# The two seams of a two-phase feed-forward: where x1 is stored from, when weights and blocks are loaded, and which buffers hold them

## The chip, the cores and the metric

The kernel runs on one core of a Trainium2 chip. The metric is device time in microseconds, from the start to the end of one execution. The core has a matrix engine (PE in the profile), a vector engine (DVE), a scalar engine (ACT), a general engine (POOL) and an engine that here only issues transfers (SP). Every engine works through its own queue in order; transfers that SP issues run on 16 DMA engines beside the others.

## The reference, cut to what matters

One layer of a streaming encoder over 1024 prompt frames and 64 sample frames (1088 tokens), model width 1024. The convolution branch, the memory branch and their merge come first; the change touches what follows:

```python
x1 = layer_norm(ALPHA * x + merged @ w_out, ln1_g, ln1_b)
ff = jnp.square(jax.nn.relu(x1 @ w_ff1)) @ w_ff2          # 1024 -> 4096 -> 1024
x2 = layer_norm(ALPHA * x1 + ff, ln2_g, ln2_b)
```

All is float32. A product is made of three passes over operands split in a high and a low part (`mm3`: high times high, high times low, low times high), so every operand has to be split once: ACT makes the high part, DVE subtracts it from the source (`split`).

## The kernel before

**Who sets the order.** The kernel is written as a Python program over symbolic tiles. A planner turns it into one fixed queue per engine: it walks a clock of its own, and whenever an engine is free in that clock it takes, among the instructions whose inputs and buffers are ready, the one that stands earliest in the program. An instruction that is ready early can so be queued far ahead of its place in the program. `pin` keeps single instructions in program order. All transfers of the kernel are issued by SP. A pool hands its buffers round; a tile waits for the last reader of the bytes that it takes over.

**Norm and first seam.** `out_proj` (L857) goes over three token chunks of 384, 384 and 320 tokens, with eight products each. For each product a slice `sx` of x is loaded back from memory (L866) and added by DVE (L872). `ln1(ci)` (L836) runs in the background, one step per product: it leaves x1 of a chunk in three tiles, the high part in pool `ph`, the low part in pool `pl` (both with three buffers, one per chunk) and the full value `Y2` in pool `f`. At its end it stores all three to memory, `y1D`, `x1Dh`, `x1Dl` (L852), because the phases after it need other shapes.

The feed-forward has 32 hidden row blocks. Four of them, units u = 0 to 3, are made the plain way (`first_units`, `unit`), 24 matmuls for each chunk, and `post_h` (L914) makes relu squared with one ACT and one DVE instruction, splits it, and stores high and low part to `hidDh`, `hidDl` (L922). Its tiles come from a ring of four (`ztile`, pool `hvs1`). Meanwhile `x1_sums` (L927) makes the four sums t1 to t4 that the fast scheme below needs, split in high and low parts, in six steps of eight DVE instructions; its two work tiles come from the same ring.

**Phase one** (`ff_first`, L1017) makes the other 28 hidden row blocks as 14 pairs (quads), q = 0 to 13. Each is a 2x2 block product in seven products instead of eight, P1 to P7. P1, P2 and P3 read parts b11, b21 and b22 of x1, which are loaded from `x1D` into the buffers of `ph` and `pl` (six transfers `xb`, L1024, in the order b11, b22, b21); P5, P6, P7 and P4 read t1, t2, t3 and t4. The order on PE is, per turn q: P6(q-1), P1(q), P7(q-1), P5(q), P4(q-1), P2(q), P3(q). The weights of a quad come as one transfer `raw` of 1 MB into a single buffer (pool `rawp`, L1037), the buffer that before held the third unit's weights; `produce` splits them in seven items, in a ring of nine (`ws`, pool `f`). ACT and DVE make seven result tiles a quad, again split, and store them to `hvD` (`put`, L1090): the operands of phase two, already in its form.

**Phase two** (`ff_second`, L1168) multiplies by `w_ff2` in seven blocks of two quads of phase one each; a block has four quads of its own (28 in all), each with seven products of twelve matmuls of 272 columns. A block's 14 operand tiles `hv` are loaded from `hvD` (`load_hv`, L1220) into one of two pools, `hvp0` for even and `hvp1` for odd blocks. The pools take bytes that phase one held. The weights of a quad are loaded by `load_w` (two buffers), split by `split_w` (three buffers). The result is accumulated by DVE in four tiles `YF` (L1244), which start as ALPHA times x1, loaded from `y1D` (L1262). The four hidden blocks of the units are multiplied at the end (`last_ff2`): `last_weights` (L1274) loads and splits their four weight tiles at the end of block 5, together with the eight halves of `hidD`. `last_ff2` turns `YF` to token-major, adds the last product, and does the final norm and the stores.

Of the kernel before, what the change touches and what calls it, by code (L numbers as in the profile page):

```python
# [9 lines left out]
F32 = mybir.dt.float32  # L10
# [39 lines left out]
def hybrid_layer(ctx, tc, x_prompt, x_sample, cache_conv, state_C, state_n, state_m, w_in, b_gate,  # L50
# [15 lines left out]
    base = ExitStack()  # L66
    ph = pool("ph", 3, stack=base)
    pl = pool("pl", 3, stack=base)
    fp = pool("f", 3, stack=base)
# [15 lines left out]
    hidD = [dram.tile([4 * P, T], F32, name=f"hidD{e}") for e in "hl"]  # L85
# [750 lines left out]
    def ln1(ci):  # L836
# [13 lines left out]
        o = CHUNKS[ci][0]  # L850
        for dst, src in ((y1D, Y2[ci]), (x1D[0], X1H[ci].bitcast(F32)), (x1D[1], X1L[ci].bitcast(F32))):
            nc.sync.dma_start(dst[:, o:o + n].rearrange("(k p) t -> p k t", p=P), src[:, :, :n])  # L852
        if ci == 2:
            lnq.close()
            lns.close()

# [57 lines left out]
    def post_h(u):  # L914
        def f(ci, o, n, ps):
            r, hi = ztile("r"), ztile("rh")
            rf = r.bitcast(F32)
            S.activation(rf[:, :n], ps[:, :n], AF.Relu)
            V.scalar_tensor_tensor(rf[:, :n], ps[:, :n], 0.0, rf[:, :n], ALU.max, ALU.mult)
            split(hi[:, :n], r[:, :n], rf[:, :n])  # L920
            for e, t in enumerate((hi, r)):
                nc.sync.dma_start(hidD[e][u * P:(u + 1) * P, o:o + n], t.bitcast(F32)[:, :n])  # L922
        return f
# [3 lines left out]
    def x1_sums():  # L927
# [4 lines left out]
        def rows(kh, i, ci, o, n):  # L932
            return Y2[ci][:, 4 * i + kh:4 * i + 4:2, o:o + n]

        for a, b, ca, oa, cb, ob in ((0, 224, 0, 0, 1, 160), (224, 384, 0, 224, 2, 0), (384, 544, 1, 0, 2, 160)):
            n = b - a
            for i in range(2):
                b11, b21, b12, b22 = rows(0, i, ca, oa, n), rows(1, i, ca, oa, n), rows(0, i, cb, ob, n), rows(1, i, cb, ob, n)
                z = [ztile("xs").bitcast(F32)[:, :2 * n].rearrange("p (k t) -> p k t", t=n) for _ in range(2)]

                def keep(nm, src):
                    hi, lo = (t[:, 2 * i:2 * i + 2, a:b] for t in XV[nm])
                    split(hi, lo, src)
                V.tensor_tensor(z[0], b11, b12, ALU.subtract)
                keep("t1", z[0])
                V.scalar_tensor_tensor(z[1], z[0], -1.0, b22, ALU.mult, ALU.subtract)
                keep("t2", z[1])
                V.tensor_tensor(z[0], b22, b12, ALU.subtract)
                keep("t3", z[0])
                V.scalar_tensor_tensor(z[1], z[1], -1.0, b21, ALU.mult, ALU.subtract)  # L950
                keep("t4", z[1])
                yield

    def first_units(u, hi, lo):
# [3 lines left out]
        if u == 1:  # L958
# [9 lines left out]
            drain("misc")  # L968
            BG["misc"].append(x1_sums())
# [47 lines left out]
    def ff_first():  # L1017
        drain("misc")
        BT = {}
# [14 lines left out]
        def produce():  # L1034
            for q in range(NQ):
                raw = pools["rawp"].tile([P, 2 * KT * P], F32R, tag="raw", name="raw").bitcast(F32)
                nc.sync.dma_start(raw.rearrange("p (k n) -> p k n", n=2 * P),  # L1037
                                  w_ff1[0][:, q * 2 * P:(q + 1) * 2 * P].rearrange("(k p) n -> p k n", p=P))
                r = raw.rearrange("p (i b n) -> p i b n", b=2, n=2 * P)
# [26 lines left out]
                item("a22", c[1, 1])  # L1066
                yield
# [92 lines left out]
        base.close()  # L1160
# [7 lines left out]
    def ff_second():  # L1168
        yp = pool("y2p")
        wr2 = pools["wr2"] = pool("wr2", 2)  # L1170
        ff2 = ExitStack()
        wv = pool("wv2", 3, stack=ff2)
        hvp = []
        stacks = [ff2, ExitStack()]
        for i in range(2):
            hvp.append(pool(f"hvp{i}", 1, stack=stacks[i]))
# [3 lines left out]
        rw, W, HV = {}, {}, {}  # L1180
# [39 lines left out]
        def load_hv(blk):  # L1220
            for nm in ("b11", "t1", "b21", "b22", "t2", "t3", "t4"):
                for k in range(2):
                    t = hvp[blk % 2].tile([P, 2, HT2], F32R, tag=f"{nm}{k}", name="hv")
                    o = ((2 * blk + k) * 7 + VN.index(nm)) * 2 * P
                    nc.sync.dma_start(t.bitcast(F32), hvD[o:o + 2 * P, :].rearrange("(e p) t -> p e t", p=P))
                    HV[blk, nm, k] = t

        def operand(q, bn, k, cs):
            t = HV[q // 4, bn, k]
            return t[:, 0, cs], t[:, 1, cs]  # L1230

        YF = [yp.tile([P, 2, T], F32, name=f"yf{j}") for j in range(4)]
# [13 lines left out]
        def between(q, nm):  # L1246
# [3 lines left out]
            if nm == "P4" and q % 4 == 3:  # L1250
                blk = q // 4
                if blk + 2 < 7:
                    load_hv(blk + 2)
                if blk == 5:
                    stacks[1].close()
                    last_weights()

        load_hv(0)
# [4 lines left out]
        split_w(0)  # L1263
        split_w(1)
        load_w(2)
        load_hv(1)
# [148 lines left out]
```

## Time and profile before

| | us |
|---|---|
| three runs | 1973.45, 1975.58, 1971.04 (median 1973.45) |
| the profiled execution | 1974.53 |
| its span in the profile | 1972.4 |
| PE busy in the span | 1893.3 (96%) |
| DVE busy | 1420.7 (72%) |
| ACT busy | 711.8 (36%) |
| POOL busy | 124.1 (6%) |

The span runs from the first to the last instruction that the profile shows; the execution's own time has some 2 us around it. The profile has a page of totals, a view of waits (who waited for whom), windows (busy time of each engine in chosen stretches, with the count of instructions in brackets, the clock granted to PE as a share of full speed, the mean busy share of the DMA engines, and GB/s), a timeline of single instructions, the chain that ended last, and the sizes of the transfers. A start time in a timeline is in us from the start of the span. "SPq" rows are transfers being issued, not carried out.

### The profile page before, as it was taken

The numbers are of one execution on the slowest core, as the hardware profiler recorded it, in microseconds if no ns is written. First come the engines' busy times: TensorE is split into PE (matmuls) and PEld (weight loads), VectorE is DVE, ScalarE is ACT, GpSimd is POOL, SyncE is SP. The second block draws the span as 40 slices with busy tenths as digits, with TensorE's granted clock in tenths as the row PEclk, the third lists the DMA queues.
The fourth block names the chain that finished last, engine by engine and source line by source line (L and its number), as shares of the span: only waits on it lengthen the run. The fifth ranks groups of instructions, "written<-read, shape, count | busy, mean of one in ns | idle before, by whom it ended". The sixth has DMA issues, their size and how long they took to land.

```text
span 1972.4 us, 31778 instructions
## 1 busy us (share of the span) xinstructions
PE 1893.3 (96%) x12732; PEld 1869.6 (95%) x12732; DVE 1420.7 (72%) x2332; ACT 711.8 (36%) x1277; POOL 124.1 (6%) x229
## 2 busy tenths in 40 slices
PE   8999999999999999999999999499999968999998
PEld 8999999999999999999999999499999968999986
DVE  4957877787688767878674467677777657777756
ACT  4333322332233223323441235466676612121123
POOL 1112210001000100000000000000000000000004
PEclk9999999999999999999999999799999989999999
DMA  4122321121112211236344234856666697676422
GB/s 143 53 79 67 110 61 44 45 78 49 55 48 74 59 55 33 67 102 209 89 123 141 68 112 166 281 184 245 231 224 247 254 397 283 214 258 251 168 104 81
DMA packets 230295, 273.77 MB, mean 139 GB/s; under 512 B 13567, under 2 KB 169711, under 8 KB 230147
## 3 DMA queue, kind: packets, MB, share of 16 engines
q1 hardware_dynamic: 230147, 271.74, 40.4%
q8 instruction: 100, 1.64, 0.3%
q14 instruction: 48, 0.39, 0.1%
HBM read 174.58 MB, written 97.05 MB: 138 GB/s over the span
## 4 chain that ended last, share of the span: by engine, by line
PE 81%; DVE 9%; DMA 7%; issue 1%; ACT 1%; SPq 0%; POOL 0%; DVEq 0%; ACTq 0%; POOLq 0%
PE g L348 17%; PE g L351 17%; PE g L352 17%; PE ya L348 4%; PE ya L352 4%; PE ya L351 4%; DMA raw<-in_w_ff_dram 2%; PE yb L348 2%; PE yb L352 2%; PE yb L351 2%; DMA hv<-hvD 1%; PE m L352 1%; PE m L348 1%; PE m L351 1%; PE yc L348 1%
## 5 line engine op out<-in xcount | busy, mean ns | idle before, releaser
L348 PE MATMUL g<-xh,wh 128*128 128x384 f32 (+1 forms) x1920 | 634.3, 330 | 0.1
L351 PE MATMUL g<-xl,wh 128*128 128x384 f32 (+1 forms) x1920 | 628.2, 327 | 0.9 <-DVE xl L180 0.9
L352 PE MATMUL g<-xh,wl 128*128 128x384 f32 (+1 forms) x1920 | 628.3, 327 | 0.0
L351 PEld LDWEIGHTS g<-xl,wh 128*128 128x128 f32 x1920 | 360.7, 188 | 1.3 <-DVE xl L180 1.2
L348 PEld LDWEIGHTS g<-xh,wh 128*128 128x128 f32 x1920 | 360.5, 188 | 0.9 <-ACT xh L179 0.4
L352 PEld LDWEIGHTS g<-xh,wl 128*128 128x128 f32 x1920 | 360.3, 188 | 0.1
L592 DVE SCALAR_TENSOR_TENSOR acc<-glu,vecs,acc 128x1118 f32<-128x1118 f32 x240 | 332.5, 1386 | 3.6
L356 ACT ACTIVATE wh<-wr 128x1024 fp32r<-128x1024 f32 (+1 forms) x167 | 144.0, 877 | 428.7 <-PE g L351 168.6
L359 DVE TENSOR_TENSOR wl<-wr,wh 128x1024 fp32r<-128x1024 f32 (+1 forms) x167 | 167.0, 1013 | 67.5 <-ACT wh L356 66.6
L348 PE MATMUL ya<-hv,wh 128*128 128x272 f32 x448 | 131.3, 294 | 23.4 <-DMA hv<-hvD 13.0
L352 PE MATMUL ya<-hv,wl 128*128 128x272 f32 x448 | 130.1, 291 | 0.5 <-DVE wl L359 0.5
L351 PE MATMUL ya<-hv,wh 128*128 128x272 f32 x448 | 129.7, 290 | 0.0
L348 PEld LDWEIGHTS ya<-hv,wh 128*128 128x128 f32 x448 | 85.9, 192 | 25.8 <-issue 13.2
L1244 DVE TENSOR_TENSOR yf<-yf,ya 128x544 f32<-128x544 f32 x100 | 70.1, 718 | 39.4 <-PE ya L352 39.1
L352 PEld LDWEIGHTS ya<-hv,wl 128*128 128x128 f32 x448 | 85.4, 191 | 0.8 <-DVE wl L359 0.7
L351 PEld LDWEIGHTS ya<-hv,wh 128*128 128x128 f32 x448 | 85.5, 191 | 0.0
L359 DVE TENSOR_TENSOR wv<-raw,wv 128x512 fp32r<-128x512 f32 x84 | 56.2, 686 | 38.1 <-ACT wv L356 37.7
L356 ACT ACTIVATE wv<-raw 128x512 fp32r<-128x512 f32 x84 | 51.0, 623 | 59.9 <-DMA raw<-in_w_ff_dram 53.9
L348 PE MATMUL g<-xh,woh 128*128 128x384 f32 (+1 forms) x192 | 63.9, 333 | 4.1 <-DVE y L872 4.1
L348 PE MATMUL yb<-hv,wh 128*128 128x272 f32 x224 | 65.0, 290 | 1.1 <-ACT wh L356 1.0
L352 PE MATMUL yb<-hv,wl 128*128 128x272 f32 x224 | 64.5, 288 | 0.5 <-DVE wl L359 0.5
L351 PE MATMUL yb<-hv,wh 128*128 128x272 f32 x224 | 64.3, 287 | 0.0
(390 smaller groups left out, 4001.1 us busy)
## 6 DMA issues: line engine op xcount, KB each, us to landing
hv<-hvD SPq DMA_DIRECT2D x98, 544.0 KB
wr<-in_w_in_dram SPq DMA_DIRECT2D x64, 512.0 KB
hvD<-zh SPq DMA_DIRECT2D x98, 272.0 KB
wr<-in_w_ff_dram SPq DMA_DIRECT2D x36, 512.0 KB
hvD<-r SPq DMA_DIRECT2D x56, 272.0 KB
raw<-in_w_ff_dram SPq DMA_DIRECT2D x14, 1024.0 KB
hvD<-t SPq DMA_DIRECT2D x42, 272.0 KB
yf<-y1D SPq DMA_DIRECT2D x4, 1088.0 KB
```

Of the source, the lines that this page charges most:

```text
L348: first = TE.matmul(out, lh, rh, start=start, stop=False, skip_group_check=more)
L351: TE.matmul(out, lh, rl, start=False, stop=False, skip_group_check=more)
L352: TE.matmul(out, ll, rh, start=False, stop=stop, skip_group_check=more)
L356: a = S.activation(hi, src, AF.Copy)
L359: V.tensor_tensor(lo, src, hi.bitcast(F32), ALU.subtract)
L592: V.scalar_tensor_tensor(acc, glu[:, j:j + AC], vecs[:, c, j:j + 1], acc, ALU.mult, ALU.add))
L1244: V.tensor_tensor(y, y, cols2(bk[b]), op)
```

## The change

Five things are changed, and no product of PE is added or taken out.

1. The stores of x1 leave `ln1`. They are written down after the norm of the last chunk, for all three chunks, in `spill_x1`, high part first and `y1D` last.
2. `post_h` makes relu and square on ACT and stores one unsplit tile; the split is done at the end, when the tile is read back (`last_hidden`). `x1_sums` works on all eight feature tiles at once, half as many instructions of twice the size, with work tiles from the weight staging pool `w` (two buffers).
3. The load of a quad's `raw` weights is written down behind the last split of the quad before (`load_raw`), and the first one ahead of the `xb` loads.
4. Pools `ph` and `pl` live on through phase two. Even blocks are loaded into their six buffers (`load_even`), block 0 from behind P3 of the last quad of phase one; odd blocks have the pool `hvp1`, loaded one tile every second product (`load_odd`). The pools of phase two are opened in another order: weights first, then `YF` (from the last to the first), then `hvp1`.
5. The four last weight tiles are loaded and split one a quad in block 6 (`last_weight`), with the first two hidden tiles; the other two hidden tiles and the tiles of the final norm go into the `ph` and `pl` buffers once block 6 is through.

```diff
+    def spill_x1(ci):
+        o, n = CHUNKS[ci]
+        for dst, src in ((x1D[0], X1H[ci].bitcast(F32)), (x1D[1], X1L[ci].bitcast(F32)), (y1D, Y2[ci])):
+            nc.sync.dma_start(dst[:, o:o + n].rearrange("(k p) t -> p k t", p=P), src[:, :, :n])
...
     def post_h(u):
         def f(ci, o, n, ps):
-            r, hi = ztile("r"), ztile("rh")
-            rf = r.bitcast(F32)
-            S.activation(rf[:, :n], ps[:, :n], AF.Relu)
-            V.scalar_tensor_tensor(rf[:, :n], ps[:, :n], 0.0, rf[:, :n], ALU.max, ALU.mult)
-            split(hi[:, :n], r[:, :n], rf[:, :n])
-            for e, t in enumerate((hi, r)):
-                nc.sync.dma_start(hidD[e][u * P:(u + 1) * P, o:o + n], t.bitcast(F32)[:, :n])
+            r = ztile("r").bitcast(F32)[:, :n]
+            S.activation(r, ps[:, :n], AF.Relu)
+            S.activation(r, r, AF.Square)
+            nc.sync.dma_start(hidD[u * P:(u + 1) * P, o:o + n], r)
...
+            z = [wpool.tile([P, KT * P], F32, tag="wr", name="xs")[:, :4 * n].rearrange("p (k t) -> p k t", t=n) for _ in range(2)]
...
             drain("misc")
+            for ci in range(3):
+                spill_x1(ci)
             BG["misc"].append(x1_sums())
...
+        load_raw(0)
         for i, (nm, kh, th) in enumerate((("b11", 0, 0), ("b22", 1, 1), ("b21", 1, 0))):
...
                 item("a22", c[1, 1])
+                load_raw(q + 1)
                 yield
...
+            if (q, nm) == (NQ - 1, "P3"):
+                load_even(0)
...
-        base.close()
+        fps.close()
...
+    HVO = [(nm, k) for nm in ("b11", "t1", "b21", "b22", "t2", "t3", "t4") for k in range(2)]
...
+    def load_even(blk):
+        big = []
+
+        def get(i):
+            while len(big) <= i:
+                big.append((ph, pl)[len(big) % 2].tile([P, 3072], F32R, tag="p", name="hv"))
+            return big[i]
+        for i, (nm, k) in enumerate(HVO):
+            if i < 12:
+                t = get(i // 2)[:, i % 2 * 2 * HT2:(i % 2 + 1) * 2 * HT2].rearrange("p (e t) -> p e t", t=HT2)
+                o = hv_row(blk, nm, k)
+                nc.sync.dma_start(t.bitcast(F32), hvD[o:o + 2 * P, :].rearrange("(e p) t -> p e t", p=P))
+                HV[blk, nm, k] = (t[:, 0], t[:, 1])
+            else:
+                pair = [get(2 * (i - 12) + e)[:, 4 * HT2:5 * HT2] for e in range(2)]
+                for e, t in enumerate(pair):
+                    o = hv_row(blk, nm, k, e)
+                    nc.sync.dma_start(t.bitcast(F32), hvD[o:o + P, :])
+                HV[blk, nm, k] = pair
...
+        wr2 = pools["wr2"] = pool("wr2", 2)
+        wv = pool("wv2", 3)
         yp = pool("y2p")
...
+        hvp1 = pool("hvp1", 1, stack=odd)
...
-        YF = [yp.tile([P, 2, T], F32, name=f"yf{j}") for j in range(4)]
+        YF = [yp.tile([P, 2, T], F32, name=f"yf{j}") for j in reversed(range(4))][::-1]
...
+            blk, n = q // 4, len(steps)
+            steps.append(nm)
+            if blk % 2 == 0 and blk < 6 and n % 28 >= 3 and (n - n % 28) // 28 == blk:
+                i = (n % 28 - 3) // 2
+                if (n % 28 - 3) % 2 == 0 and i < 12:
+                    load_odd(blk + 1, i)
...
+            if nm == "P4" and q % 4 == 3 and blk % 2 == 0 and blk + 2 < 7:
+                load_even(blk + 2)
+            if nm == "P2" and blk == 6:
+                last_weight(q % 4)
...
-        load_hv(0)
         load_w(0)
         load_w(1)
         for j in range(4):
             nc.sync.dma_start(YF[j], y1D[j * 2 * P:(j + 1) * 2 * P, :].rearrange("(b p) t -> p b t", p=P))
-        split_w(0)
-        split_w(1)
-        load_w(2)
-        load_hv(1)
+            if j == 0:
+                split_w(0)
+                split_w(1)
+                load_w(2)
...
+    def last_hidden(k, hi, lo, raw):
+        nc.sync.dma_start(raw, hidD[k * P:(k + 1) * P, :])
+        for x in (hi, lo):
+            G.memset(x[:, T:].bitcast(F32), 0.0)
+        split(hi[:, :T], lo[:, :T], raw)
+        HID[k] = (hi, lo)
+
+    def last_weight(k):
+        la = pools["la"]
+        raw = pools["wr2"].tile([P, KT * P], F32, tag="wr", name="wr")
+        nc.sync.dma_start(raw, w_ff2[0, (28 + k) * P:(29 + k) * P, :])
+        WH.append(la.tile([P, D], F32R, name=f"w2h{k}"))
+        WL.append(la.tile([P, D], F32R, name=f"w2l{k}"))
+        split(WH[k], WL[k], raw)
+        if k < 2:
+            last_hidden(k, la.tile([P, TW], F32R, name=f"hid{k}h"), la.tile([P, TW], F32R, name=f"hid{k}l"),
+                        la.tile([P, T], F32, tag="hidr", name="hidr"))
...
+        big = [pp.tile([P, 3072], F32, tag="p", name="big") for pp in (ph, pl, pl, ph)]
+        for k in range(2, 4):
+            t = (ph, pl)[k % 2].tile([P, 3072], F32R, tag="p", name="hid")
+            last_hidden(k, t[:, 0:TW], t[:, TW:2 * TW], big[0][:, (k - 2) * T:(k - 1) * T])
```

More of the change, by code (lines that the diff above doesn't have):

```diff
@@ L84, in hybrid_layer @@
     x1D = [dram.tile([D, T], F32, name=f"x1D{e}") for e in "hl"]
-    hidD = [dram.tile([4 * P, T], F32, name=f"hidD{e}") for e in "hl"]
+    hidD = dram.tile([4 * P, T], F32, name="hidD")
     hvD = dram.tile([14 * 7 * 2 * P, 544], F32, name="hvD")
@@ L930, in x1_sums, with rows, keep @@
             XV[nm] = [tv.tile([P, 4, HT2], F32R, tag=nm + e, name="x" + nm + e) for e in "hl"]
-        def rows(kh, i, ci, o, n):
-            return Y2[ci][:, 4 * i + kh:4 * i + 4:2, o:o + n]
+        def rows(kh, ci, o, n):
+            return Y2[ci][:, kh:KT:2, o:o + n]
         for a, b, ca, oa, cb, ob in ((0, 224, 0, 0, 1, 160), (224, 384, 0, 224, 2, 0), (384, 544, 1, 0, 2, 160)):
             n = b - a
[L937 to L952, printed above, removed]
+            b11, b21, b12, b22 = rows(0, ca, oa, n), rows(1, ca, oa, n), rows(0, cb, ob, n), rows(1, cb, ob, n)
+            z = [wpool.tile([P, KT * P], F32, tag="wr", name="xs")[:, :4 * n].rearrange("p (k t) -> p k t", t=n) for _ in range(2)]
+            def keep(nm, src):
+                split(*(t[:, :, a:b] for t in XV[nm]), src)
+            V.tensor_tensor(z[0], b11, b12, ALU.subtract)
+            keep("t1", z[0])
+            V.scalar_tensor_tensor(z[1], z[0], -1.0, b22, ALU.mult, ALU.subtract)
+            keep("t2", z[1])
+            yield
+            V.tensor_tensor(z[0], b22, b12, ALU.subtract)
+            keep("t3", z[0])
+            V.scalar_tensor_tensor(z[1], z[1], -1.0, b21, ALU.mult, ALU.subtract)
+            keep("t4", z[1])
+            yield
     def first_units(u, hi, lo):
@@ L1168, in ff_second @@
     def ff_second():
+        wr2 = pools["wr2"] = pool("wr2", 2)
+        wv = pool("wv2", 3)
         yp = pool("y2p")
[L1170 to L1176, printed above, removed]
+        odd = ExitStack()
+        hvp1 = pool("hvp1", 1, stack=odd)
         banks = ExitStack()
@@ L1218, in weight, with load_odd @@
             return tuple(t[:, i * P:(i + 1) * P] for t in W[q])
[L1220 to L1226, printed above, removed]
+        def load_odd(blk, i):
+            nm, k = HVO[i]
+            t = hvp1.tile([P, 2, HT2], F32R, tag=f"{nm}{k}", name="hv")
+            o = hv_row(blk, nm, k)
+            nc.sync.dma_start(t.bitcast(F32), hvD[o:o + 2 * P, :].rearrange("(e p) t -> p e t", p=P))
+            HV[blk, nm, k] = (t[:, 0], t[:, 1])
         def operand(q, bn, k, cs):
-            t = HV[q // 4, bn, k]
-            return t[:, 0, cs], t[:, 1, cs]
-        YF = [yp.tile([P, 2, T], F32, name=f"yf{j}") for j in range(4)]
+            hi, lo = HV[q // 4, bn, k]
+            return hi[:, cs], lo[:, cs]
+        YF = [yp.tile([P, 2, T], F32, name=f"yf{j}") for j in reversed(range(4))][::-1]
         def done(q, nm, bk):
```

67 lines of the change are left out of this document (29 added, 38 removed).

## The prediction, made before the changed kernel was run

> **What bounds the kernel now.** I read the page first, then PE's waits, then windows around the places where PE stops.
>
> ```profile
> span 1972.4 us, 31778 instructions
> ```
> ```profile
> PE ya L348 <- ACT wv L356: 28.0, 1, 28.0
> PE ya L348 <- DMA hv<-hvD: 13.0, 1, 13.0
> PE g L348 <- DVE y L872: 4.1, 1, 4.1
> ```
> ```profile
> 1163.00:1175.00 12.00, 12.00 (x84) 12.00 (x83) 11.74 (x16) 9.76 (x14) 0.00 (x0) 1.00 0.28 107
> 1175.00:1181.00 6.00, 5.16 (x36) 4.90 (x34) 3.67 (x6) 2.01 (x2) 0.00 (x0) 1.00 1.06 397
> 1181.00:1186.40 5.40, 0.94 (x7) 0.77 (x7) 2.31 (x6) 0.52 (x1) 1.00 (x2) 0.89 0.93 321
> 1186.40:1192.40 6.00, 6.00 (x24) 6.00 (x25) 2.03 (x5) 0.00 (x0) 0.00 (x0) 0.53 0.18 56
> 1249.30:1277.40 28.10, 0.16 (x2) 0.00 (x0) 14.22 (x31) 9.90 (x22) 0.00 (x0) 0.57 0.89 303
> 1277.40:1281.00 3.60, 3.55 (x16) 3.53 (x17) 3.54 (x6) 2.06 (x4) 0.00 (x0) 0.53 0.03 7
> 1577.70:1590.80 13.10, 0.19 (x2) 0.00 (x0) 11.36 (x21) 6.59 (x12) 0.00 (x0) 0.63 1.01 369
> 1590.80:1609.00 18.20, 17.86 (x119) 16.84 (x120) 6.24 (x9) 0.00 (x0) 0.00 (x0) 0.89 1.04 407
> 1609.00:1637.00 28.00, 18.93 (x135) 17.13 (x134) 12.59 (x20) 2.52 (x4) 0.00 (x0) 0.98 1.01 391
> 1637.00:1651.00 14.00, 13.78 (x88) 13.54 (x88) 11.53 (x23) 4.40 (x8) 0.00 (x0) 0.80 0.69 235
> 1700.00:1750.00 50.00, 50.00 (x402) 50.00 (x402) 39.17 (x65) 9.80 (x15) 0.00 (x0) 1.00 0.71 257
> ```
>
> PE is the bound nearly everywhere: 402 matmuls in 50 us is 0.124 us each, without a hole, and the change takes no matmul away. Only places where PE does less can be won. With 0.124 us a matmul (84 in 12 us, 0.143, at the norm) a window's loss is its length less count times price. **At the norm** (1175 to 1192.4): 0.9 + 4.4 + 2.6 = 7.8 us. **First seam**: 27.9 + 1.6 = 29.5. **Second seam** (1577.7 to 1651): 12.9 + 3.4 + 11.3 + 3.1 = 30.7. Together 68 us; this is the most that the change can bring.
>
> **The norm's place.** The chain of waits, and SP's timeline around it:
>
> ```profile
> 1173.73 12.09 DMA sx<-xTD
> 1246.74 7.57 DMA hidDh<-rh
> 1269.87 6.87 DMA raw<-in_w_ff_dram
> ```
> ```profile
> 4.23 2.47 SPq L241 DMA_DIRECT2D fa<-in_w_in_dram  x1
> 10.70 2.27 SPq L163 DMA_DIRECT2D x<-in_x_prompt_dram  x4
> ...
> 1170.84 0.37 SPq L852 DMA_DIRECT2D y1D<-y  x1
> 1173.14 0.55 SPq L852 DMA_DIRECT2D x1Dl<-x1l  x1
> 1173.73 13.43 SPq L866 DMA_DIRECT2D sx<-xTD  x6
> ...
> 1247.88 0.41 SPq L1024 DMA_DIRECT2D xb<-x1Dh  x1
> 1252.72 0.32 SPq L922 DMA_DIRECT2D hidDh<-rh  x1
> 1255.77 0.43 SPq L1024 DMA_DIRECT2D xb<-x1Dl  x1
> ```
>
> Three stores of chunk 0 go out by 1173.14; the small load sx behind them lands 12.09 us later, and DVE, then PE, wait for it. Does writing the stores later in the program move them? The planner goes by readiness: L241, which stands behind all of the x loads, was queued at 4.23, ahead of four of them at 10.70. So the stores will not wait for the norm's end; a gap on SP lets them out. But they now rank behind sx. That rank counts in the planner's clock, too: the two halves of one xb, ready together, stand at 1247.88 and 1255.77 with a higher-ranked hidden store between them, so SP was busy there and rank decided. I expect one store, not three, ahead of each sx: some 4 of the 12 us. PE's wait of 4.14 us and its slow restart go, 1.5 us stays: **6.3 us gained**. Bounds: 0 (order unchanged) and 7.8.
>
> **The first seam.** PE ends the units at 1249.3. What was late is the last row of the chain: raw, issued at 1269.87 behind the last hidden store, 6.87 us to land. Ahead of it the posts were late, since hidden tiles wait for their stores in a ring of four (7.57 us). Removed from DVE: the square and the split's subtraction of each post, and half of x1_sums' instructions:
>
> ```profile
> 1233.92 1.23 DVE L359 TENSOR_TENSOR wl<-wr,wh 128x1024 fp32r<-128x1024 f32 x1 [0.46 <-ACT wh L356]
> 1235.60 0.62 DVE L359 TENSOR_TENSOR xt4l<-xs,xt4h 128x448 fp32r<-128x448 f32 x1
> ```
>
> Between these rows an instruction of 896 costs about 1.1 us, one of 640 about 0.8: 8 x 1.1 + 16 x 0.8 = 21.6 us. Added wait: the second work tile takes the staging buffer of the fourth unit's weights, free when their split ends (1233.92 + 1.23). Queued behind that wait on DVE are the rest of the sums; from 1235, t1 of the third group is done 8.8 + 6.4 + 2 later, at 1252. P5(0), its reader, is PE's second product of 3 us (24 x 0.124), so from 1252.3: just covered. Posts sit on ACT alone, two instructions each, and their ring of four now holds one tile a post, so eight posts need four turns of it, not sixteen.
>
> What is late next is transfers:
>
> ```profile
> x1Dh<-x1h SPq DMA_DIRECT2D x1, 1280.0 KB
> xb<-x1Dh SPq DMA_DIRECT2D x3, 1088.0 KB
> raw<-in_w_ff_dram SPq DMA_DIRECT2D x14, 1024.0 KB
> hidDh<-rh SPq DMA_DIRECT2D x8, 192.0 KB
> hv<-hvD SPq DMA_DIRECT2D x98, 544.0 KB
> ```
>
> From 1230 the queue must carry the last chunk's three stores (3840 KB), raw (1024), six xb (6528) and some eight hidden stores (about 1440): 12832 KB = 13.1 MB. The windows above show 303 to 407 GB/s; I take 370: 35 us, so b21 lands at 1265. b11, third in line (8 MB), lands at 1251.7. PE idles 3 us, makes P1 and P5 until 1259, takes P3 (b22) to 1262, waits for b21 until 1266: 7.5 us idle and two slow restarts of 1.6 (the row of 1277.4): 11 of 29.5 stay, **18.5 us gained**. Bounds by the rate alone: 303 gives 19 left, 407 gives 7.
>
> Here the Trainium skill speaks against it ("DMA: Bandwidth & Descriptors", section "Where 436 GB/s comes from"): transfers between device memory and SBUF are bound at about 358 GB/s for a core. By that b21 comes at 1266.6, 1.2 us later. The trace disagrees (407 in the window from 1590.8), and the measurement decides.
>
> **The raw loads in phase one** move one item, some 3 us, forward in SP's queue. PE loses nothing there now; I put 0 on them and keep a rival.
>
> **The second seam.** hv of block 0 went out at 1585.59, after the last result stores; PE waited for it 13.0 us, then ran hand to mouth with the DMA engines full until 1637.
>
> ```profile
> 1585.59 13.36 SPq L1225 DMA_DIRECT2D hv<-hvD  x14
> ```
> ```profile
> 1551.00:1561.00 10.00, 9.98 (x80) 9.76 (x79) 6.41 (x10) 6.01 (x11) 0.00 (x0) 1.00 0.40 154
> 1561.00:1577.70 16.70, 15.01 (x118) 14.54 (x116) 7.88 (x12) 9.45 (x16) 0.00 (x0) 1.00 0.92 345
> ```
> ```profile
> 1579.35 0.68 DVE L359 TENSOR_TENSOR wl<-wr,wh 128x512 fp32r<-128x512 f32 x1
> 1586.70 2.43 DVE L359 TENSOR_TENSOR wl<-wr,wh 128x1024 fp32r<-128x1024 f32 x2
> ```
>
> In the changed kernel block 0 goes into the buffers of b11, b21 and b22, which P1, P2 and P3 of the last quad free before 1566.5; only P6, P7 and P4 follow. A third of its 7.8 MB (14 x 544 KB) fits into the 10 us from 1551, where the engines are 60% idle, the rest competes with result stores and arrives in the order of use. So hv is off the path. Next late are the weights: their split waits for bytes that phase one's weight ring holds until P4(13) ends at 1577.7, and stands beside the last results on DVE, as now: first part at 1580, the sums' part at 1587.9 (first of the two at 1586.70). Between them PE has three products of 12 matmuls that need the first part alone, 4.5 us. Idle: 2.3 + 3.2. Then YF and the rest of the transfers: block 0 to the end of the odd block's loads still needs the same bytes, begun some 10 us earlier; I put 4 us on that and 3 us on two slow restarts: 12.5 of 30.7 stay, **18 us gained**. Bounds: 6 left (only the split) and 22 left (the old middle, 11.3 + 3.1, and a pause of 7).
>
> PE's clock: after the idle 27.9 us it ran at 0.53 for 3.6 us, after 4.14 us of idling likewise, while pauses near 1 us (1609 to 1637) left it at 0.98. The Trainium skill ("TensorE: Matmul & The Clock Gate", section "What's actually happening") puts the limit at an idle window of about 3.4 us; by it my pauses of 2 to 4 us may each escape, which is a rival below.
>
> **The tail.** Two hidden tiles are now read and split (DVE 1.23 us each, as above for 1024) only once block 6 frees `ph` and `pl`:
>
> ```profile
> 1907.88 0.48 PE L348 MATMUL po<-w2h,hid0h 128*128 128x512 f32 x1
> ```
>
> The first two tiles and eight transposes give PE about 2.5 us of cover after P4(27); the second split ends about 4 us after it (ACT ahead of the first, then two on DVE). Cost 1.5 us; bounds 0 and 5 (read only then). The last weights, one a quad, cost the same work beside PE: 0.
>
> **Sum.** 6.3 + 18.5 + 18 - 1.5 = 41 us. From the profiled execution's 1974.5 (span 1972.4) that is 1933; the median of three runs lies 1.1 lower: **1932 us**.
>
> **Rivals.**
> - The stores keep their old places: the order at the norm is as before, 6.3 us are not won. 1938. For it: readiness did put them there; against: rank decided elsewhere. Chance 0.20.
> - The stores do come behind the norm: nine of them, 13.4 MB, then raw, xb and hidden stores, 22.5 MB from 1230 at 370 GB/s: b11 at 1278, b21 at 1291. The first seam gets 6 us worse, which eats the norm's gain; 18 - 1.5 stay: 1957. Chance 0.13.
> - The remaining pauses stay short: no slow restarts and 400 GB/s; 6 and 5.5 us more are won at the two seams: 1921. Chance 0.15.
> - Slower: raw loads, now earlier on SP, wait there for the last split with result stores queued behind them; result tiles come free later, ACT and DVE stop, then PE, in all 13 further quads. The trace has this wait today:
>
> ```profile
> SPq L1037 <- DVE wv L359: 28.7, 13, 8.1
> ```
>
>   2.2 us each, hidden. If the move lets 4 us a quad through to PE, 13 x 4 = 52 us are lost: 1984; it is slower from 41 / 13 = 3.2 us on. Against it: PE has no hole there, and the planner still queues by readiness. Chance 0.07.
> - No measurable difference, by such losses of half that size: 0.03.
>
> **Chances.** The forecast itself has 0.42 (1920 to 1946). The range reaches to the short pauses and the late stores with their bounds: 1913 to 1958. A measurement can tell about 0.2% (4 us) from no change: faster 0.90, same 0.03, slower 0.07.
>
> **What would show it.** Right: sx rows between the store rows at the norm and no wait for L872; raw issued before the xb rows; the longest PE wait at the first seam under 6 us and put down to xb; hv of block 0 issued from about 1551 on and PE's first wait of phase two put down to weight splits; a short wait for a hidden split before po. Wrong: three stores in a row before sx; nine stores after 1230; holes of PE inside phase one; PE holes at the starts of odd blocks, where `load_even` sends 7.8 MB at once and a weight load queues behind it.

## The result and the profile after

| | median us | runs | lowest to highest | span of the profiled run |
|---|---|---|---|---|
| before | 1974.51 | 4 | 1971.04 to 1975.62 | 1972.4 |
| changed | 1942.26 | 4 | 1939.93 to 1943.65 | 1941.1 |

The ratio is 0.9838, 95% interval 0.9821 to 0.9855: 1.6% less, 32 us. The forecast was 1932 us, 1913 to 1958: the time lies in the range, 10 us above the forecast.

Four events in PE's timeline say where. Start of the first matmul of P1(0): 1277.45 before, 1248.39 after. Last matmul of phase one: 1577.61 and 1552.10. First matmul of the tail (`pt`): 1906.82 and 1875.02. End: 1972.4 and 1941.1. So 25.5 us are won up to the end of phase one, 6.3 more in phase two, and 0.5 is lost in the tail: 31.3 in all, the difference of the spans. Line numbers from here on are those of the changed kernel or of the experiment's own, except where the kernel before is named.

PE's waits in the changed kernel (us in all, times, longest):

```profile
PE ya L348 <- ACT wh L356: 20.4, 1, 20.4
...
PE ya L348 <- DMA xb<-x1Dh: 5.0, 1, 5.0
```

The wait of 28.0 us at the first seam became one of 5.0, and it is put down to x1's loads. The wait for y at the norm is gone. But at the second seam a wait of 20.4 us for the weight split stands where 13.0 us for hv stood: it is longer than the one it replaced. The windows of the changed kernel (busy time of PE, PEld, DVE, ACT and POOL, granted clock, share of the DMA engines, GB/s):

```profile
1175.00:1192.40 17.40, 16.64 (x115) 16.38 (x114) 13.76 (x23) 5.91 (x9) 1.00 (x2) 1.00 0.80 282
...
1243.20:1248.40 5.20, 0.18 (x3) 0.04 (x1) 5.20 (x9) 4.37 (x9) 0.00 (x0) 0.95 0.97 314
1248.40:1256.00 7.60, 5.94 (x27) 5.31 (x28) 5.99 (x10) 2.41 (x4) 0.00 (x0) 0.59 1.04 406
...
1552.20:1572.80 20.60, 0.20 (x3) 0.02 (x1) 4.49 (x8) 3.74 (x8) 0.00 (x0) 0.57 1.05 405
1572.80:1577.00 4.20, 4.20 (x18) 4.20 (x19) 4.12 (x10) 1.95 (x4) 0.00 (x0) 0.50 0.89 367
1577.00:1600.00 23.00, 23.00 (x179) 23.00 (x177) 20.10 (x34) 5.48 (x9) 0.00 (x0) 0.96 0.85 316
```

With the prices of the prediction the losses are 17.4 - 115 x 0.143 = 1.0 us at the norm (7.8 before), 12.8 - 30 x 0.124 = 9.1 at the first seam (29.5), and 20.2 + 2.0 + 0.8 = 23.0 at the second (30.7). The second seam has changed its shape: all the loss is now the pause and the slow restart; the holes from 1609 to 1651 before, 11.3 + 3.1 us, are gone. By these windows the three places win 34.9 us, by the events 31.3; the difference was lost outside the windows (0.5 of it in the tail) and was not followed further.

The norm's order, in SP's timeline of the changed kernel:

```profile
1172.00 0.37 SPq L857 DMA_DIRECT2D y1D<-y  x1
1172.42 3.81 SPq L868 DMA_DIRECT2D sx<-xTD  x4
1176.28 0.49 SPq L857 DMA_DIRECT2D x1Dh<-x1h  x1
1179.45 2.46 SPq L868 DMA_DIRECT2D sx<-xTD  x2
1181.96 0.43 SPq L857 DMA_DIRECT2D x1Dl<-x1l  x1
```

The stores are still issued here, though they are written behind the norm; but one store, not three, stands ahead of each group of sx. And the second seam, from the chain of waits and from SP's timeline:

```profile
1543.58 7.73 DMA hv<-hvD
1551.32 8.73 DMA hv<-hvD
1560.12 5.70 DMA hvD<-zh
1565.88 6.20 DMA wr<-in_w_ff_dram
1572.10 0.64 ACT wh L356
```
```profile
1541.28 0.41 SPq L1096 DMA_DIRECT2D hvD<-t  x1
1541.79 6.17 SPq L1187 DMA_DIRECT2D hv<-hvD  x8
1548.63 4.35 SPq L1193 DMA_DIRECT2D hv<-hvD  x4
1554.06 0.32 SPq L1096 DMA_DIRECT2D hvD<-zh  x1
...
1565.16 0.32 SPq L1096 DMA_DIRECT2D hvD<-t  x1
1565.88 1.04 SPq L1217 DMA_DIRECT2D wr<-in_w_ff_dram  x2
```

Block 0's last twelve transfers leave SP at 1541.79 to 1553; not one result store leaves it in these 12 us. Fourteen stores follow from 1554.06 to 1565.16, and behind them the two weight loads that PE waits for, at 1565.88, 13.8 us after PE's last product. In the kernel before, SP's timeline has the same two loads 9.6 us ahead of PE's last product (1577.61):

```profile
1567.99 0.99 SPq L1186 DMA_DIRECT2D wr<-in_w_ff_dram  x2
```

### The profile page after: what moved, and what is told of

Same layout as the page of the kernel before. It is cut to its first block, busy times and chain, and to the rows that moved or that the text cites. A ratio compares the mean times of both kernels' runs of the same rounds, so it can differ in the third digit from the quotient of the medians.

```text
span 1941.1 us, 31659 instructions
## 1 busy us (share of the span) xinstructions
PE 1888.6 (97%) x12732; PEld 1867.1 (96%) x12732; DVE 1409.2 (73%) x2288; ACT 712.9 (37%) x1269; POOL 124.8 (6%) x229
## 4 chain that ended last, share of the span: by engine, by line
PE 90%; DVE 4%; DMA 3%; issue 1%; ACT 1%; POOL 0%; DVEq 0%; SPq 0%; POOLq 0%; ACTq 0%
PE g L348 18%; PE g L351 18%; PE g L352 18%; PE ya L348 5%; PE ya L352 5%; PE ya L351 5%; PE yb L348 3%; PE yb L352 3%; PE yb L351 3%; PE yc L348 1%; PE yc L351 1%; PE yc L352 1%; PE m L348 1%; PE m L352 1%; PE m L351 1%; DMA hv<-hvD 1%
## 5 line engine op out<-in xcount | busy, mean ns | idle before, releaser
L348 PE MATMUL ya<-hv,wh 128*128 128x272 f32 x448 | 130.0, 290 | 23.6 <-ACT wh L356 20.4
```

Source lines behind the costliest of these rows:

```text
L348: first = TE.matmul(out, lh, rh, start=start, stop=False, skip_group_check=more)
```

## The experiments

**Theory after the result.** The gains of the norm and the first seam are what the prediction says they are. The second seam failed since the weight loads are late, and they are late by their rank on SP, that is by their place in its queue (behind block 0 and the stores). **Rivals:** by memory (the change gave the raw weight buffers other bytes, which come free late), or by bytes (the DMA engines are full, 405 GB/s in the pause, and any order ends at the same time). Each ratio is against runs of the kernel before on the same chip; between two rows the ratios compare better than the medians. "Ends phase one" and "begins phase two" are the starts of PE's last and first matmul in the profiled run.

| kernel | median us | ratio, 95% interval | ends phase one | begins phase two | span |
|---|---|---|---|---|---|
| stores alone | 1966.81 | 0.9964 (0.9951 to 0.9976) | 1571.27 | 1584.67 | 1963.8 |
| stores and raw loads | 1958.44 | 0.9917 (0.9904 to 0.9931) | 1562.93 | 1576.20 | 1955.1 |
| changed, old post work | 1945.42 | 0.9848 (0.9835 to 0.9862) | 1557.01 | 1577.29 | 1942.9 |
| changed | 1942.26 | 0.9838 (0.9821 to 0.9855) | 1552.10 | 1572.79 | 1941.1 |
| changed, hidden stores by ACT | 1936.13 | 0.9810 (0.9796 to 0.9824) | 1548.50 | 1568.60 | 1934.3 |
| block 0 behind the weights | 1940.96 | 0.9830 (0.9816 to 0.9843) | 1552.92 | 1568.17 | 1939.9 |
| memory order alone | 1939.55 | 0.9819 (0.9805 to 0.9832) | 1554.81 | 1556.33 | 1938.9 |
| weights early | 1934.64 | 0.9800 (0.9786 to 0.9814) | 1551.04 | 1561.87 | 1933.4 |
| weights early, block 0 late | 1935.64 | 0.9799 (0.9786 to 0.9812) | 1550.34 | 1554.19 | 1933.9 |
| the same, one ring, y1 first | 1929.98 | 0.9773 (0.9759 to 0.9786) | 1549.39 | 1553.24 | 1926.7 |
| the same, own slots | 1930.77 | 0.9776 (0.9762 to 0.9789) | 1549.55 | 1553.40 | 1927.9 |
| own slots, hidden stores by ACT | 1930.00 | 0.9771 (0.9758 to 0.9785) | 1548.85 | 1552.70 | 1928.2 |
| memory order, block 0 late, ACT | 1931.55 | 0.9778 (0.9765 to 0.9791) | 1549.52 | 1551.03 | 1930.4 |

### The norm: the stores' place alone

The kernel before, with this part of the change and no other:

```diff
-        for dst, src in ((y1D, Y2[ci]), (x1D[0], X1H[ci].bitcast(F32)), (x1D[1], X1L[ci].bitcast(F32))):
...
+            for ci in range(3):
+                spill_x1(ci)
             BG["misc"].append(x1_sums())
```

> The kernel before with one part of the change: the stores of x1 and y1 written in order high, low, y behind the norm's last chunk. Theory of the prediction (the loss of 7.8 us at the norm is the loads of x held behind stores, and one store ahead of each in place of three leaves 1.5 of it; the first seam does not gain from it): 6 to 7.5 us less than before, 1966 to 1968.5 us, ratio 0.9963 to 0.9970. Rival (the norm's hole comes from elsewhere, or the stores are only shifted into the first seam): 0 to 2 us less, 1972 to 1975.

Measured 1966.81, 7.0 us less than before (1973.76 in this comparison). Windows and waits of this kernel:

```profile
1175.00:1192.40 17.40, 16.64 (x115) 16.37 (x114) 13.74 (x24) 6.37 (x10) 1.00 (x2) 1.00 0.78 271
```
```profile
PE ya L348 <- ACT wv L356: 27.3, 1, 27.3
```

115 matmuls stand in the norm's window as in the changed kernel, and the first seam's wait is still 27.3 us. So the norm's gain comes from this part alone, and the first seam neither adds to it nor takes it back.

### The first seam, in two steps

The same kernel, with the raw loads moved as the change moves them:

```diff
+        load_raw(0)
         for i, (nm, kh, th) in enumerate((("b11", 0, 0), ("b22", 1, 1), ("b21", 1, 0))):
...
                 item("a22", c[1, 1])
+                load_raw(q + 1)
```

> The kernel before with two parts of the change: the stores' place, and the raw weight loads of phase one ahead of the loads of x1 (quad 0's) and one item earlier (the others'). With the stores alone TensorE still waits 27.28 us at the first seam, put down to the weight split; that run's median is 1966.8. Theory (the raw load's place in SyncE's queue is the last link of this wait, the loads of x1 the next): TensorE waits 12 to 20 us, now for the loads of x1, and the kernel takes 8 to 14 us less than with the stores alone, 1953 to 1959. Rival (the posts hold everything: a ring of four with two tiles and two stores a post): the raw load goes out earlier, but the loads of x1 land as late as before or later; 0 to 4 us less, 1963 to 1967.

Measured 1958.44; phase one ends 8.3 us earlier than with the stores alone. Waits, and SP's timeline, of this kernel:

```profile
PE ya L348 <- DVE r L921: 16.2, 1, 16.2
```
```profile
1236.18 0.40 SPq L1028 DMA_DIRECT2D raw<-in_w_ff_dram  x1
1236.68 0.64 SPq L1036 DMA_DIRECT2D xb<-x1Dh  x1
...
1240.26 0.46 SPq L1036 DMA_DIRECT2D xb<-x1Dl  x1
```

The raw load left SP at 1236.18 in place of 1261.88 with the stores alone (1269.87 before), and the time came as expected. But what PE waits for next is not x1, as the theory had it: it is a post on DVE (L921), and the loads of b11 were on their way at 1240. So the post's chain seems to be a bound of its own. The changed kernel with the old post work (relu squared on VectorE, two tiles of the ring a post) tests that:

```diff
-            r = ztile("r").bitcast(F32)[:, :n]
...
-            S.activation(r, r, AF.Square)
...
+            r, hi = ztile("r"), ztile("rh")
...
+            V.scalar_tensor_tensor(rf[:, :n], ps[:, :n], 0.0, rf[:, :n], ALU.max, ALU.mult)
+            nc.sync.dma_start(hidD[u * P:(u + 1) * P, o:o + n], rf[:, :n])
+            split(hi[:, :n], r[:, :n], rf[:, :n])
```

> The changed kernel with the post work of the four first units put back on VectorE (relu squared by a product with the matmul's sum, then the split) with two tiles of the ring of four a post; the hidden tile is still stored once. Theory (at the first seam the loads of x1 decide, the post's work has no part): the wait for x1's loads stays at 5 us within 1.5; 1940.5 to 1944. Rival (the shorter post is what lets the stores and loads go out early): the wait grows by 4 to 12 us, 1946 to 1954.

Measured 1945.42. The two intervals overlap, so the medians do not settle it; the trace does: PE's waits at this seam are then

```profile
PE ya L348 <- DVE r L921: 6.3, 1, 6.3
PE yc L351 <- DMA xb<-x1Dl: 2.4, 1, 2.4
PE yb L348 <- DVE r L921: 1.7, 1, 1.7
```

and phase one ends 4.9 us later than in the changed kernel. The median lies between the two forecasts (1940.5 to 1944 and 1946 to 1954), and the first wait grew by 1.3 us, not by 4 or more; but PE now waits for the post, twice, and not for the first load of x1. So the rival has the mechanism, at a smaller size. By the ends of phase one the 25.5 us are 6.3 for the stores' place, 8.3 for the raw loads, 4.9 for the post's work, and 5.9 for what stands between the second and third row of the table (one store a hidden tile, x1's sums in half as many instructions, and the parts of the change in phase two), which was not tried alone.

What is left there? In the changed kernel the first load of x1 leaves SP at 1242.65, behind three hidden stores that hold SP from 1238.62 for 3.94 us; four more held the raw load before that:

```profile
1228.35 6.10 SPq L921 DMA_DIRECT2D hidD<-r  x4
1234.86 0.38 SPq L1024 DMA_DIRECT2D raw<-in_w_ff_dram  x1
1238.62 3.94 SPq L921 DMA_DIRECT2D hidD<-r  x3
1242.65 0.38 SPq L1032 DMA_DIRECT2D xb<-x1Dh  x1
```

With the hidden stores, twelve in all, issued by ScalarE:

```diff
-            nc.sync.dma_start(hidD[u * P:(u + 1) * P, o:o + n], r)
+            nc.scalar.dma_start(hidD[u * P:(u + 1) * P, o:o + n], r)
```

> The changed kernel with the stores of the hidden tiles issued by ScalarE's queue instead of SyncE's. In the changed kernel the first load of x1 is issued at 1242.65 us, behind three hidden stores on SyncE, and TensorE waits 5.02 us for it. Theory (order on SyncE): the load goes out up to 3.9 us earlier, the wait falls to 1 to 3 us, 1938 to 1940.5 us. Rival (the buffers of x1, or the bytes ahead of it, set its time): the wait stays within 1 us, 1941 to 1944. ScalarE's instructions at this place take longer by the issue; a store there that waits would hold the posts behind it, seen as a slower seam.

SP's timeline and two windows of this run:

```profile
1234.44 0.36 SPq L1032 DMA_DIRECT2D xb<-x1Dh  x1
1235.97 0.36 SPq L1032 DMA_DIRECT2D xb<-x1Dl  x1
```
```profile
1243.70:1246.80 3.10, 0.36 (x2) 0.16 (x2) 3.10 (x6) 1.89 (x5) 0.00 (x0) 0.78 1.04 407
1246.80:1252.00 5.20, 5.20 (x23) 5.20 (x24) 5.20 (x9) 1.97 (x4) 0.00 (x0) 0.50 1.04 405
```

The first load leaves 8.2 us earlier (6.9 against the end of the units, which lies 1.3 earlier in this run), more than the three stores' 3.9: the raw load ahead of it already leaves 4.6 us earlier (1230.28). The waits fall to 1.58 and 2.74 us. The median is 1936.13, 6.1 us less than the changed kernel and below the theory's 1938 to 1940.5, though the two intervals still touch. Of this the end of phase one shows 3.6; of the rest, 1.6 is a shorter wait for the accumulation in `YF` in phase two (3.2 and 1.6 us in all), and the remainder was not traced to a place. During what remains of the waits the DMA engines are full (405 to 407 GB/s), which points to bytes; no run took bytes away.

### The second seam: rank, memory or bytes

Block 0's loads, written behind the two weight loads:

```diff
-            if (q, nm) == (NQ - 1, "P3"):
-                load_even(0)
...
         load_w(0)
         load_w(1)
+        load_even(0)
```

> The changed kernel with block 0's sixteen loads written behind the first two weight loads of phase two instead of beside phase one's last products. In the changed kernel TensorE waits 20.4 us at this seam (1552.10 to 1572.79), the fourteen last result stores go out between 1554.06 and 1565.5, and the first weight load behind them at 1565.88. Theory (rank on SyncE: the loads of block 0 hold the stores, the stores hold the weights): the stores are no longer held, the first weight load goes out 4 to 8 us earlier against the last product of phase one, and so does the restart; 1934 to 1939 us. Rival (memory: the weight buffers come free only then, whatever stands ahead): the weight load goes out some 13 to 14 us behind the last product as now, and SyncE waits at it; 1940 to 1944. Rival (bytes: the transfers are saturated and set the restart in any order): the weight load may go out earlier but lands no earlier, or block 0 lands later by as much; 1940 to 1946.

```profile
1560.45 0.40 SPq L1096 DMA_DIRECT2D hvD<-t  x1
1560.94 1.62 SPq L1215 DMA_DIRECT2D wr<-in_w_ff_dram  x2
```
```profile
PE ya L348 <- ACT wh L356: 15.0, 1, 15.0
...
PE ya L348 <- DVE yf L1270: 4.3, 1, 4.3
```

The last store and the weight load behind it leave SP some 5 us earlier, and the wait falls from 20.4 to 15.0: block 0's loads did hold the queue. But a new wait of 4.3 us for y1, whose load now stands behind block 0's, takes most of it back, and the median (1940.96, where the theory had 1934 to 1939) can't be told from that of the changed kernel. The rank behind block 0 is thus a part of it, and no more.

The weight loads beside the last quads: they go into phase one's weight ring, made of two 4 KB buffers that phase two keeps. For the space, the ring of result tiles has 13 in place of 14.

```diff
+            if (q, nm) == (NQ - 1, "P1"):
+                first_w(0, RW)
+                first_w(1, RW)
...
-        wr2 = pools["wr2"] = pool("wr2", 2)
...
-                rw[q] = wr2.tile([P, KT * P], F32, tag="wr", name="wr")
...
+        rw[q] = wpool.tile([P, KT * P], F32, tag="wr", name="wr")
```

> The changed kernel with the first two weight loads of phase two written beside P1 of the last pair of quads. They go to phase one's weight ring, which for that is made of two 4 KB buffers that phase two keeps; the result tiles' ring has 13 tiles for 14, three of them in the memory of the first quad's raw weights. Block 0's loads stay where the change put them. Theory (rank): the weights land well ahead of the last product, and the wait of 20.4 us for the weight split falls to 3 to 10 us (the split can begin when the last product has left the weights' memory, and takes some 3 us); 1928 to 1936 us. The stores are still held behind block 0's loads, which now costs TensorE nothing. Rival (memory): the same, as these buffers come free early. Rival (bytes): the restart stays within 3 us of where it is, with the wait put down to block 0's loads; 1939 to 1944. A cost that no theory asks for: a smaller ring can stop phase one, seen as holes ahead of 1540 us.

> Both edits in one: weights beside the last quads, block 0's loads written behind them at the start of phase two. Theory (rank): as with the weights alone the first matmul of phase two comes 4 to 11 us behind the last product of phase one; the stores end earlier, but the second half of block 0 lands later, so that products of the first quad wait for it; between 3 us faster and 4 us slower than the weights alone, 1926 to 1938 us. Rival (bytes): 1939 to 1946.

Measured 1934.64 with early weights, 1935.64 with block 0 late besides. The waits of the first are

```profile
PE ya L348 <- ACT wh L356: 10.5, 1, 10.5
...
PE yb L348 <- ACT wh L356: 4.5, 1, 4.5
```

With both edits PE restarts 3.85 us after its last product in place of 20.7, and the time is the same as with the weights alone: three waits of 3.6, 4.2 and 4.3 us (split, sums' split, y1) stand in the first 24 us. Both times lie where the theory put them, though the first wait with early weights is longer than its 3 to 10 us. There the held stores still cost PE time: ACT stood 6.71 us, until 1559.94, for a result tile whose store had not landed, and the weight split came behind that on ACT. That a restart 7.7 us sooner wins nothing can mean that bytes bound the seam from here on, or that the next waits in line are again a matter of order and memory. The first of the combined runs below speaks for the second.

Is the lateness in the changed kernel rank or memory? Nothing is moved in the program here; only the buffers of phase two lie in another order, so that the raw weight buffers take over the bytes of phase one's raw weights and not those of its split weights:

```diff
+        wv = pool("wv2")
+        pool("gap").tile([P, 256], F32, name="gap")
         wr2 = pools["wr2"] = pool("wr2", 2)
-        wv = pool("wv2", 3)
+        wl2 = pool("wl2")
         yp = pool("y2p")
...
-            hi, lo = (wv.tile([P, 14 * P], F32R, tag="w" + e, name="w" + e) for e in "hl")
+            hi, lo = ((wl2 if (q % 3, e) == (2, "l") else wv).tile([P, 14 * P], F32R, tag=f"w{e}{q % 3}", name="w" + e) for e in "hl")
```

> The changed kernel with nothing moved in its program; only the order of phase two's buffers in memory is another: split weights first, then the two raw weight buffers, which so come to lie where phase one keeps its raw weights (last read by the last quad's seventh weight item, some 25 us ahead of the last product) and not in its split weights (read until the last product). Theory (memory decides the time of the weight loads; the order on SyncE behind stores and block 0's loads is only what follows from it): the first weight load goes out ahead of 1540 us with no edit of its place, TensorE's wait of 20.4 us falls to 8 to 13 us as in the run with early weights, 1932 to 1937 us. Rival (the rank of the weight loads, written after phase one's last product, keeps them behind the last stores): the load goes out at 1565 as before, 1940 to 1945 us.

```profile
1529.12 0.38 SPq L1219 DMA_DIRECT2D wr<-in_w_ff_dram  x1
...
1567.74 0.32 SPq L1096 DMA_DIRECT2D hvD<-t  x1
1568.39 0.38 SPq L1219 DMA_DIRECT2D wr<-in_w_ff_dram  x1
```
```profile
PE ya L348 <- ACT wh L356: 10.5, 2, 9.2
...
PE yb L348 <- ACT wh L356: 2.3, 1, 2.3
```

The first weight load goes out at 1529.12 instead of 1565.88 with no edit of its place, and phase two begins 1.5 us after phase one. So memory decided the first load's time. The second quad's load, whose buffer lies in the same tile of phase one, still stands behind the stores, at 1568.39, and PE waits 9.2 us for the split that needs it: that one is rank, since with block 0 written later, in the last run below, both loads go out together at 1523.82:

```profile
1523.82 1.98 SPq L1217 DMA_DIRECT2D wr<-in_w_ff_dram  x2
```

The theory's numbers missed (1932 to 1937 expected, 1939.55 measured). It took both loads to go early; and phase one ends 2.7 us later in this run, some 2 of them between 1475 and 1525 (381 matmuls, 398 in the changed kernel), for a reason that was not traced.

Then the pieces together, from the kernel with early weights and late block 0. First all split weights in one ring with y1's first load ahead of block 0's rest, then these weights at fixed places, then that with the hidden stores on ScalarE:

```diff
-        wv = pool("wv2", 3)
+        wv = pool("wv2", 6)
...
-            hi, lo = (wv.tile([P, 14 * P], F32R, tag="w" + e, name="w" + e) for e in "hl")
+            hi, lo = (wv.tile([P, 14 * P], F32R, tag="w", name="w" + e) for e in "hl")
...
-        load_even(0)
...
             if j == 0:
+                load_even(0)
```

> The kernel with early weights and late block 0, with two more edits: the split weights of phase two in one ring of six (so that the first two quads' lie in the memory of phase one's weights and not of its result tiles), and the first load of y1 written ahead of block 0. With early weights and late block 0 alone TensorE waits 3.56, 4.25 and 4.33 us (weight split, sums' split, y1) in the first 24 us of phase two. Theory (order and memory, piece by piece): the second wait goes since its split waited for result stores to leave the memory, the third falls to under 2; 1928 to 1932 us. Rival (bytes: the stores, block 0, y1 and block 1 are one saturated stretch, and a wait that goes comes back later): 1933 to 1937.

```diff
-        wv = pool("wv2", 6)
+        wv = pool("wv2", 1)
...
-            hi, lo = (wv.tile([P, 14 * P], F32R, tag="w", name="w" + e) for e in "hl")
+            hi, lo = (wv.tile([P, 14 * P], F32R, tag=f"w{e}{q % 3}", name="w" + e) for e in "hl")
```

> Early weights, late block 0 and y1 ahead of its rest, with the six split-weight tiles of phase two at fixed places (high and low of the quads 0 and 1 first, in the memory of phase one's weights) in place of a ring. In the ring of six VectorE waited 5.67 us for a store of a result tile before it could write the first low part, and TensorE 6.49 us for it; 1930.0 us. Theory (that wait was memory that the low part shared with result tiles): it goes, and TensorE's waits in the first 24 us of phase two sum to under 6 us after the first of 3.6; 1925 to 1929 us. Rival (bytes: the stretch of transfers from 1540 to 1585 us sets when the first block can be worked on, and the wait moves to block 0's loads or y1): 1929 to 1932.

> The same with the hidden stores on ScalarE's queue. With the hidden stores there alone the changed kernel lost 3 to 6 us less at the first seam (waits of 1.58 and 2.74 us in place of 5.02, 1.34 and 0.33; 1936.1 against 1942.3). Theory (the two seams are independent): 4 to 6 us less than the run beside it, 1920 to 1925 us. Rival (what is won at the first seam is given back at the second): within 2 us of the run beside it.

The times are 1929.98, 1930.77 and 1930.00: one time. The first is where its theory (order and memory) put it, and 5.7 us below the run that it starts from, with intervals that just touch: order and memory were still worth something, though the DMA engines were full there too. Its waits moved: that for y1 fell from 4.3 to 0.4 us, that for the sums' split is gone, and a longer one for a low part of the weights stands in its place:

```profile
PE ya L352 <- DVE wl L359: 6.5, 1, 6.5
```

VectorE stood 5.67 us for a store whose bytes this low part took over, and PE 6.49 us for it. At fixed places that wait is 0.73 us, and 4.13 us for y1 take its place; with the hidden stores on ScalarE phase one ends 0.7 us earlier and the wait for y1 is 6.2. Windows of the run with fixed places:

```profile
1549.60:1553.40 3.80, 0.24 (x2) 0.02 (x1) 3.70 (x6) 3.49 (x7) 0.00 (x0) 1.00 0.95 330
1553.40:1567.60 14.20, 9.33 (x49) 8.90 (x49) 8.61 (x18) 3.21 (x5) 0.00 (x0) 0.76 1.03 391
1567.60:1585.00 17.40, 17.00 (x121) 16.78 (x122) 11.40 (x19) 2.95 (x5) 0.00 (x0) 0.90 1.04 407
```

From 1553 to 1585 the DMA engines are full at 391 and 407 GB/s. In both later runs the rival's time came true. With fixed places the wait moved to y1, as the rival (bytes) has it; that bytes are the bound is argued from the full engines, for no run moved fewer of them. With the stores on ScalarE little was won at the first seam in the first place (waits of 2.20 and 2.79 us for 4.16 and 1.20), and those 0.7 us were lost again in the wait for y1. The last run takes the memory order, with phase one's rings as the change has them:

> That memory order, with block 0's loads written behind the first load of y1, and the hidden stores on ScalarE's queue; phase one's rings are those of the change. Theory (what is left at the second seam is bytes: stores, half of block 0 and y1, as in the runs at 1930): TensorE waits about 3.6 us for the first split, under 1 for its low part, and 4 to 7 us for y1; 1926 to 1931 us. Rival (the gains of the two seams add up since phase one's rings are not cut here): 1920 to 1926.

1931.55, again the same time and half a microsecond above the theory's range; the rival (the gains add up) is out. Phase two begins 1.5 us after phase one, sooner than the 3.6 us of the theory, and waits of 0.8 to 3.5 us follow down the line. This version differs from the changed kernel in the memory order above, the place of `load_even(0)` behind y1's first load, and one word for the queue of the hidden stores; at a ratio of 0.9778 it beats both kernels, 0.6% (some 12 us) ahead of the change.

## Why the prediction was right or wrong

**The norm, 6.3 us: right, by its own mechanism.** The loss fell from 7.8 to 1.0, and the stores' place alone gives 7.0 us. The order on SP is the one forecast: readiness still puts the stores there, rank puts one ahead of each group of sx. The rivals on the stores (old places; nine of them behind the norm) did not happen: the last chunk's stores left SP by 1227.7.

**The first seam, 18.5 us: the sum right by luck, its parts not.** 19.2 came (25.5 less the 6.3 of the stores' place). The prediction left 7.5 us of idling, 3 of them for b11 and the rest for b21, and two slow restarts. Measured were 5.0 us for b11, no wait for b21, and one slow restart: the units ended 6 us earlier through the norm's gain (1243 and not 1249), which the step took no account of, and b11 arrived at 1248.4, three us ahead of the 1251.7. These errors of either sign cancel. That raw was last in line and the posts next was right, as the two runs show; transfers came only third. Here the clock would not have spared the short pauses, which was a rival (0.15): with the hidden stores on ScalarE, pauses of 1.58 and 2.74 us still left the clock at 0.50 for 5.2 us. The Trainium skill ("TensorE: Matmul & The Clock Gate", section "What's actually happening") puts the limit at an idle window of about 3.4 us that runs freely; two pauses below it, two matmuls apart, make 4.3 us, and the trace fits such a window better than a limit for a single pause.

**Raw loads in phase one, 0: right.** In the changed kernel's phase one the five windows of 50 us from 1275 to 1525 hold 397 to 401 matmuls, about as many as before (397 to 402 from 1300 to 1550), and from 1256 to its end PE's waits name nothing over 0.9 us. The rival on the other side (4 us a quad, 1984) did not happen.

**The second seam, 18 us: wrong; 6.3 came.** The step that failed is "hv is off the path. Next late are the weights: their split waits for bytes that phase one's weight ring holds until P4(13) ends", with 2.3 + 3.2 us of idling and 4 for the rest. That hv is off the path and that PE's first wait is put down to the weight split were right, and so was the memory: but it held the raw load, not the split alone. The step took the load as landed, as in the kernel before, where it was issued 9.6 us ahead of PE's last product. The diff opens `wr2` first of phase two's pools, in the bytes of the split weights, so the load could not start ahead of that product (with the order of the buffers changed and nothing else, it left at 1529.12); by then it ranked behind fourteen result stores, and these behind twelve loads of block 0, which the change itself had sent early. One pause of 20.4 us came from it, where the step had 2.3. The other part of the step was too dark: the holes behind the restart, put at 4 us, are 0.8; that block 0 and most of the rest landed during the pause, at 405 GB/s, is the likely reason, and no run tried it.

**The tail, -1.5: -0.5.** From the first `pt` to the end it is 66.1 us after 65.6; no hidden split is waited for. This was read from the two traces alone; no run tried it apart.

## What to carry to other kernels

When a load is to hide behind the end of a stage, two dates count besides its place in the program: when the last reader leaves the bytes that its buffer takes over, and what already stands ahead of it in the issuing queue; a change of the order in which pools are opened moves the first without moving any instruction. An in-order issuing queue turns a load that was sent early into a wait for the stores behind it, and these into a wait for whatever comes after them; so each step that sends bytes early is to be followed down the queue to the next small transfer that something waits for. Where the DMA engines are full across a seam, a wait that is removed can hand its time to the next transfer in line, as in the last four versions here, all within 1.6 us; so add up the bytes of the seam before choosing an order. Full engines alone don't say that order is done: with them full, order and memory were still worth 5.7 us (1935.64 to 1929.98).

## What the runs showed of the hardware

- The transfers ran at 391 to 422 GB/s in windows with the DMA engines full (391 and 407 with fixed places, 405 in the pause at 1552, 422 in the window below, of the run with weights early and block 0 late). The Trainium skill ("DMA: Bandwidth & Descriptors", section "Where 436 GB/s comes from") has about 358 as the limit of one core between device memory and SBUF, half of what two cores share. Only one core runs here, and the measurement decides; no run here shows two.

```profile
1573.90:1580.00 6.10, 6.10 (x30) 6.10 (x31) 4.86 (x10) 2.00 (x3) 0.00 (x0) 0.57 1.02 422
```

- A second issuing queue was worth more than its issue time. The Trainium skill ("DMA: Bandwidth & Descriptors", section "Issuing engines are not separate DMA queues") says that other engines' queues save only the time to start a transfer. Here twelve small stores on ScalarE's queue let the first load of x1 go 8.2 us earlier: in the changed kernel SP waits for the hidden tiles' data at these stores, and everything behind a store waits with it (6.10 and 3.94 us in the rows above, for seven stores, where the median store of this kind leaves in 0.33 us). The kernel took 6.1 us less. On the version with fixed places the same edit gave nothing (1930.77 and 1930.00).
